# A state-space stage: per-head scalings as copies on ScalarE

## The chip, the cores and the metric

The kernel runs on one core of one Trainium2 chip. The metric is device time in microseconds; lower is better. The core has TensorE (matmuls), VectorE, ScalarE, GpSimd and SyncE, each with an instruction queue of its own that runs in order.

## The reference, cut to what matters

One layer of a hybrid encoder for a prompt of 1024 frames and for a running stream of 32 frames. One input projection feeds a state-space group of 8 heads (64 wide, two groups of four heads that share B and C of 128) and an attention group of 8 heads; both are joined by an output projection and followed by a gated feed-forward block.

```python
dt = softplus(dt_raw + dt_bias);  a = -exp(a_log)
da_cum = cumsum(dt * a)                               # inside a chunk
decay[q, s] = exp(da_cum[q] - da_cum[s])  for s <= q  # per head
scores = einsum('cqhn,cshn->cqsh', cm, bm) * decay
y_diag = einsum('cqsh,cshp->cqhp', scores, x * dt)
y_off  = einsum('cqhn,chpn,cqh->cqhp', cm, h_prev, exp(da_cum))
y = y_diag + y_off + d_skip[:, None] * xs
y = rmsnorm(y * silu(z), ssd_norm_g)
q, k = rmsnorm(q, q_norm_g), rmsnorm(k, k_norm_g)     # per head of 64
```

## The kernel before, in words

All matmuls that need it are made from two float32r halves, a rounded one and the rest, so each weight or activation is split: a cast to float32r and a subtraction. `split_unit` does that for weights, with the cast on ScalarE (L138) and the subtraction on GpSimd (L139).

The stage of interest runs from about 195 to 380 us. It merges two tracks, `merge(pieces[1:SSD_PIECES], chunks + ...)` (L618):

- `pieces`: the projection to v, k and q, by half and by pairs of 128-row tiles. A piece runs 2 x 24 matmuls of 256 columns into one of two PSUM banks of the tag "mm" (L153 to L155); ScalarE copies the bank to SBUF (L490). For q and k `qk_pair` then normalizes by head: square on ScalarE (L434), sum on VectorE (L436), `rsqrt` on GpSimd (L145, L146), two products on VectorE (L438, L439), and the split into `il`: the rounded half by a cast on GpSimd (L448), the rest by a subtraction on GpSimd (L449). One step later TensorE transposes `il` (L457), ScalarE copies the result to `st` (L460), and it is stored to DRAM for attention. v pieces are stored as they are.
- `chunks`: nine chunks of the scan, 128 rows each (the ninth is the stream's 32 rows). A chunk has five steps, one per turn, so that several chunks are under way. Step 1 loads `xb`, `bc`, `zz` and makes four `dm` tiles (128 x 4 x 128, float32r) on GpSimd: `upper`, the triangle of ones, times a per-partition, per-head scalar of `dAh` or `dAl` (L541). Step 2 sums them with `lowr` on TensorE (L548), takes the exponential on ScalarE (L551), masks the scores (L556, L560), and makes `xdt` on VectorE (L562), `xde` on GpSimd (L564) and `xd` on GpSimd: the inputs times `d_skip` of their head (L566). Steps 3 to 5 make the state (L575 to L589), the output (L595 to L602) and its transpose (L606 to L614).

`dm` has four buffers, just one chunk's worth, so a chunk's first `dm` waits for L548 of the chunk before; `xd` has two. Pools and buffers are given out by the Tile framework, which also sets each engine's order: it orders the instructions by a simulated timeline with the program's order as priority, and puts in the waits. DMAs are issued by SyncE. After the stage the remaining pieces (k and q of the second half) are merged with attention.

Of the kernel before, what the change touches and what calls it, by code (L numbers as in the profile page):

```python
# [7 lines left out]
F32 = mybir.dt.float32  # L8
# [3 lines left out]
AF = mybir.ActivationFunctionType  # L12
ALU = mybir.AluOpType
AX = mybir.AxisListType

P = 128
# [27 lines left out]
def build(tc, a):  # L44
    nc = tc.nc
# [26 lines left out]
    def nm(s):  # L72
        cnt[0] += 1
        return f"{s}_{cnt[0]}"
# [3 lines left out]
    def bank(tag, dt=F32):  # L78
        return ps.tile([P, 1024 if tag == "s" else 512], dt, tag=tag, bufs=BUFS[tag], name=nm("ps_" + tag))
# [62 lines left out]
    def rsqrt(pl, ss, n, rows, cols):  # L142
        m = pl.tile([P, cols], F32, tag=f"rs_m{cols}", bufs=2, name=nm("rs_m"))[:rows]
        r = pl.tile([P, cols], F32, tag=f"rs_r{cols}", bufs=2, name=nm("rs_r"))[:rows]
        nc.gpsimd.tensor_scalar(m, ss, 1.0 / n, EPS, op0=ALU.mult, op1=ALU.add)  # L145
        nc.gpsimd.tensor_tensor(r, m, mhalf[:rows, 0:cols], op=ALU.pow)  # L146
        return r

    def bc3(v, n):
        return v.unsqueeze(2).broadcast_to([v.shape[0], v.shape[1], n])  # L150
# [111 lines left out]
    dtb, alog, dsk = crow[:, 0:8], crow[:, 8:16], crow[:, 16:24]  # L262
# [19 lines left out]
    upper = cq.tile([P, P], F32, name="upper")  # L282
# [145 lines left out]
    def qk_pair(raw, tp, rows, g, hs, is_k):  # L428

        nt = raw.shape[1]  # L430
        r3 = raw.rearrange("p t h d -> p (t h) d")
        sq = p1.tile([P, 512], F32, tag="sq", bufs=1, name=nm("sq"))
        s3 = sq[:rows, 0:nt * 256].rearrange("p (h d) -> p h d", d=64)
        nc.scalar.activation(s3, r3, AF.Square)  # L434
        ss = p1.tile([P, 8], F32, tag="ss8", name=nm("ss8"))
        nc.vector.tensor_reduce(ss[:rows, 0:4 * nt], s3, axis=AX.X, op=ALU.add)  # L436
        r = rsqrt(p1, ss[:rows, 0:4 * nt], 64, rows, 4 * nt)
        nc.vector.tensor_tensor(r3, r3, bc3(r, 64), op=ALU.mult)  # L438
        nc.vector.tensor_tensor(r3, r3, g[:rows].unsqueeze(1).broadcast_to([rows, 4 * nt, 64]), op=ALU.mult)  # L439
        hc = slice(hs * 256, hs * 256 + 256)  # L440
        if is_k:
            if nt == 1:
                nc.sync.dma_start(a["o_ks"][:, hc], raw.rearrange("p t h d -> p (t h d)"))
            elif tp >= 2:
                nc.sync.dma_start(a["o_kp"][(tp - 2) * 256:(tp - 1) * 256, hc].rearrange("(t p) c -> p t c", p=P),
                                  raw.rearrange("p t h d -> p t (h d)"))
        il = p1.tile([P, 8, 2, 64], F32R, tag="il", name=nm("il"))
        nc.gpsimd.tensor_copy(il[:rows, 0:4 * nt, 0, :], r3)  # L448
        nc.gpsimd.tensor_tensor(il[:rows, 0:4 * nt, 1, :], r3, il[:rows, 0:4 * nt, 0, :], op=ALU.subtract)  # L449
        yield  # L450
        st = p1.tile([P, 4, 2 * P], F32R, tag="st", name=nm("st"))
        sf = st.bitcast(F32)
        hd = slice(4 * hs, 4 * hs + 4)
        for k in range(nt):
            tb = bank("t", F32R)
            for j in range(4):
                nc.tensor.transpose(tb[:, j * rows:(j + 1) * rows],  # L457
                                    il[:rows, 4 * k + j, :, :].rearrange("p a d -> p (a d)"), idr[:rows, :rows])
            tv = tb[:, 0:4 * rows].rearrange("p (j c) -> p j c", j=4)
            nc.scalar.copy(out=st[:, :, k * rows:(k + 1) * rows], in_=tv)  # L460
        c0, n = (2 * tp * P, 2 * P) if nt == 2 else (SB, NS)
        if is_k:
            nc.sync.dma_start(kst_d[hd, :, c0:c0 + n].rearrange("h p c -> p h c"), sf[:, :, 0:n])
        else:
            nc.sync.dma_start(qst_d[:, hd, 0, c0:c0 + n], sf[:, :, 0:n])
            nc.sync.dma_start(qst_d[0:64, hd, 1, c0:c0 + n], sf[64:128, :, 0:n])
            nc.sync.dma_start(qst_d[64:128, hd, 1, c0:c0 + n], sf[0:64, :, 0:n])

    class Slot:
# [10 lines left out]
        def piece(self, tp):  # L480
            hs, kind = self.hs, self.kind
            hc = slice(hs * 256, hs * 256 + 256)
            if tp == 4:
                rw, rows = self.rs, NS
            else:
                pb = bank("mm")
                for k in range(2):
                    tok_gemm(self.units, pb, 2 * tp + k, 256 * k)
                rw, rows = p1.tile([P, 2, 4, 64], F32, tag="raw", name=nm("rw")), P
                nc.scalar.copy(out=rw.rearrange("p t h d -> p (t h d)"), in_=pb)  # L490
            if tp == 2 and self.next:
                self.next.load()
            if kind:
                yield from qk_pair(rw, tp, rows, gk if kind == 1 else gq8, hs, kind == 1)
                return
            rf = rw.rearrange("p t h d -> p t (h d)")
            if tp == 4:
                nc.sync.dma_start(v_d[SB:NT, hc], rf[:, 0, :])
                nc.sync.dma_start(a["o_vs"][:, hc], rf[:, 0, :])
            else:  # L500
                pt_ = "(t p) c -> p t c"
                nc.sync.dma_start(v_d[tp * 256:(tp + 1) * 256, hc].rearrange(pt_, p=P), rf)
                if tp >= 2:
                    nc.sync.dma_start(a["o_vp"][(tp - 2) * 256:(tp - 1) * 256, hc].rearrange(pt_, p=P), rf)
# [16 lines left out]
    def v3(x_):  # L521
        return x_.rearrange("p (h d) -> p h d", h=8)

    def ssd_chunk(c):
        rows = P if c < 8 else NS
# [10 lines left out]
        xs = xb[:, 0:512]  # L536
        dms = []
        for d in (dAh, dAl):
            for g in range(2):
                dm = p3.tile([P, 4, P], F32R, tag="dm", bufs=4, name=nm("dm"))  # L540
                nc.gpsimd.tensor_tensor(dm, upper.unsqueeze(1).broadcast_to([P, 4, P]),  # L541
                                        bc3(d[:, c, 4 * g:4 * g + 4], P), op=ALU.mult)
                dms.append(dm)
        yield
        sg = bank("s")
# [17 lines left out]
        xde = p3.tile([P, 512], F32, tag="xde", bufs=1, name=nm("xde"))  # L563
        nc.gpsimd.tensor_tensor(v3(xde), v3(xdt), bc3(de[:, c, :], 64), op=ALU.mult)  # L564
        xd = p3.tile([P, 512], F32, tag="xd", name=nm("xd"))
        nc.gpsimd.tensor_tensor(v3(xd), v3(xs), bc3(dsk, 64), op=ALU.mult)  # L566
        yield
        if c == 8:
            st_in = p3.tile([P, 512], F32, tag="h", name=nm("h"))
# [45 lines left out]

    states = {-1: None}
    chunks, chunks_end = pipelined([ssd_chunk(c) for c in range(9)])
    merge(pieces[1:SSD_PIECES], chunks + [lambda: None])  # L618
    chunks_end()
# [695 lines left out]
```

## Time and profile before

| | |
|---|---|
| median of 3 runs | 1361.01 us (1359.01 to 1367.7) |
| profiled execution | 1365.81 us, span 1364.1 us |
| mean granted TensorE clock | 0.977 |
| TensorE busy | 1286.8 us (94%) |
| VectorE busy | 904.8 us (66%) |
| ScalarE busy | 502.6 us (37%) |
| GpSimd busy | 616.6 us (45%) |

How to read it: times of rows are those of one profiled execution. PE is TensorE's matmuls, PEld its weight loads, DVE is VectorE, ACT ScalarE, POOL GpSimd. A matmul's recorded time covers its pipelined run, so consecutive matmuls overlap in the record and a busy TensorE is not one at its peak. Idle time counts only on an engine that others wait for. Waits are put down to what released them last.

### The profile page before, as it was taken

Reading aid. Unit: us, or ns where it says so; the run is one execution under the profiler, and the core shown is the slowest. Engines: PE = TensorE matmul, PEld = TensorE weight load, DVE = VectorE, ACT = ScalarE, POOL = GpSimd, SP = SyncE. Lnnn points to the kernel's source line nnn. Section 1 sums busy time; section 2 is a strip of 40 time slices with the busy share of each in tenths; the row PEclk is TensorE's granted clock in tenths of the full one; section 3 lists DMA queues with packets and bytes.
Section 4 is the critical chain, followed back from the end, with each engine's and each line's share of the span. In section 5 each row is a group of like instructions: output and inputs, shape, how many; then the busy total and the mean of one; then the engine's idle time right before and its main releaser. Section 6 shows DMA issues by size and latency. Waiting matters only on the chain.

```text
span 1364.1 us, 23795 instructions
## 1 busy us (share of the span) xinstructions
PE 1286.8 (94%) x9260; PEld 1172.2 (86%) x9260; DVE 904.8 (66%) x1271; ACT 502.6 (37%) x865; POOL 616.6 (45%) x507
## 2 busy tenths in 40 slices
PE   5999999977899899999599999999999997999998
PEld 4999999967888688688599999999999995777777
DVE  5346446785747555665966677676676766667886
ACT  6235332322237543553533343333343335111210
POOL 7142248987636210220324455434455433345585
PEclk9999999978999999999799999999999999999999
DMA  7265252445375987665134454444454468668755
GB/s 270 76 206 161 90 171 66 151 134 182 121 212 178 335 285 225 194 202 173 68 94 136 146 171 139 131 136 133 148 171 138 132 213 295 234 229 306 254 189 204
DMA packets 201600, 242.02 MB, mean 177 GB/s; under 512 B 25840, under 2 KB 163120, under 8 KB 201488
## 3 DMA queue, kind: packets, MB, share of 16 engines
q1 hardware_dynamic: 201488, 240.51, 55.0%
q8 instruction: 73, 1.20, 0.4%
q14 instruction: 39, 0.32, 0.1%
HBM read 149.47 MB, written 90.99 MB: 176 GB/s over the span
## 4 chain that ended last, share of the span: by engine, by line
PE 66%; POOL 7%; DVE 7%; DMA 6%; issue 6%; ACT 1%; SPq 1%; DVEq 0%; ACTq 0%; POOLq 0%
PE ps_w L970 33%; PE ps_z L1171 11%; PE ps_mm L153 3%; PE ps_mm L154 3%; PE ps_mm L155 3%; PE ps_mm L162 2%; PE ps_mm L160 2%; PE ps_mm L161 2%; PE ps_mm L734 1%; PE ps_t L717 1%; POOL dm L541 1%; PE ps_s L695 1%; DMA qst_d<-st 1%; POOL rs_r L146 1%; DVE Z L1176 1%
## 5 line engine op out<-in xcount | busy, mean ns | idle before, releaser
L970 PE MATMUL ps_w<-T,whi 128*128 128x264 f32 x1408 | 229.5, 285 | 6.6 <-ACT T L918 5.9
L970 PEld LDWEIGHTS ps_w<-T,whi 128*128 128x128 f32 x1408 | 195.6, 189 | 7.2 <-ACT T L918 6.3
L978 DVE TENSOR_TENSOR sc<-sc,ps_w 128x528 f32<-128x528 f32 x154 | 105.3, 698 | 75.9 <-PE ps_w L970 73.9
L153 PE MATMUL ps_mm<-whi,hT_hi 128*128 128x256 f32 (+1 forms) x512 | 149.9, 293 | 5.5 <-ACT hT_hi L227 3.3
L155 PE MATMUL ps_mm<-whi,hT_lo 128*128 128x256 f32 (+1 forms) x512 | 149.4, 292 | 0.4 <-DVE hT_lo L228 0.4
L154 PE MATMUL ps_mm<-wlo,hT_hi 128*128 128x256 f32 (+1 forms) x512 | 149.3, 292 | 0.0
L970 PE MATMUL ps_w<-T,wlo 128*128 128x264 f32 x704 | 144.3, 287 | 0.0
L139 POOL TENSOR_TENSOR wlo<-raw,whi 128x1024 fp32r<-128x1024 f32 (+1 forms) x32 | 80.9, 2537 | 136.1 <-ACT whi L138 124.7
L946 ACT CAST whi<-raw 128x1024 fp32r<-128x1024 f32 x88 | 82.7, 941 | 99.7 <-PE ps_w L970 85.0
L1176 DVE TENSOR_TENSOR Z<-ps_z,Z 128x512 f32<-128x512 f32 x140 | 92.8, 685 | 37.2 <-PE ps_z L1171 30.5
L970 PE MATMUL ps_w<-fA,whi 128*128 128x264 f32 x704 | 116.3, 288 | 0.0
L947 DVE TENSOR_TENSOR wlo<-raw,whi 128x1024 fp32r<-128x1024 f32 x88 | 107.6, 1225 | 6.2 <-ACT whi L946 3.9
L1013 DVE TENSOR_TENSOR sc<-sc 128x512 fp32r<-128x512 f32 x77 | 77.7, 1019 | 48.7 <-ACT sc L1012 26.5
L970 PEld LDWEIGHTS ps_w<-T,wlo 128*128 128x128 f32 x704 | 109.8, 190 | 0.0
L153 PEld LDWEIGHTS ps_mm<-whi,hT_hi 128*128 128x128 f32 x512 | 100.2, 196 | 7.1 <-ACT hT_hi L227 3.7
L155 PEld LDWEIGHTS ps_mm<-whi,hT_lo 128*128 128x128 f32 x512 | 100.4, 196 | 1.8 <-DVE hT_lo L228 0.8
L154 PEld LDWEIGHTS ps_mm<-wlo,hT_hi 128*128 128x128 f32 x512 | 100.1, 196 | 0.3
L970 PEld LDWEIGHTS ps_w<-fA,whi 128*128 128x128 f32 x704 | 99.8, 191 | 0.4 <-PE ps_w L1064 0.4
L1171 PE MATMUL ps_z<-whi,fA 128*128 128x512 f32 x276 | 97.5, 391 | 0.0
L1012 ACT CAST sc<-sc 128x512 fp32r<-128x512 f32 x77 | 46.8, 621 | 111.5 <-DVE sc L1002 69.9
L954 POOL TENSOR_TENSOR raw<-raw,raw 128x512 f32<-128x512 f32 x22 | 37.2, 1690 | 91.1 <-DVE wlo L947 91.1
L970 PE MATMUL ps_w<-fA,wlo 128*128 128x264 f32 x352 | 72.2, 287 | 0.0
(284 smaller groups left out, 3099.6 us busy)
## 6 DMA issues: line engine op xcount, KB each, us to landing
act_d<-sc SPq DMA_DIRECT2D x154, 256.0 KB, 2.9
fA<-act_d SPq DMA_DIRECT2D x36, 896.0 KB, 6.3
raw<-in_wgu_dram SPq DMA_DIRECT2D x44, 512.0 KB, 3.6
raw<-in_wd_dram SPq DMA_DIRECT2D x22, 512.0 KB, 4.4
x<-in_xp_dram SPq DMA_DIRECT2D x16, 512.0 KB, 7.1
q<-qst_d SPq DMA_DIRECT2D x32, 256.0 KB, 4.6
mx<-mix_d SPq DMA_DIRECT2D x16, 512.0 KB, 4.5
raw<-in_wq_dram SPq DMA_DIRECT2D x14, 512.0 KB, 4.8
```

Of the source, the lines that this page charges most:

```text
L139: (eng or nc.gpsimd).tensor_tensor(lo, raw, hi, op=ALU.subtract)
L153: nc.tensor.matmul(ps_, lhsT=lh, rhs=rh, start=start, stop=False)
L154: nc.tensor.matmul(ps_, lhsT=lh, rhs=rl, start=False, stop=False)
L155: nc.tensor.matmul(ps_, lhsT=ll, rhs=rh, start=False, stop=stop)
L946: nc.scalar.copy(out=t[0][:, 0:w], in_=src)
L947: nc.vector.tensor_tensor(t[1][:, 0:w], src, t[0][:, 0:w], op=ALU.subtract)
L970: nc.tensor.matmul(out[:, h, :], lhsT=A[x][:, kb, :], rhs=B[:, y, kb, h * Q:(h + 1) * Q], start=(n == 0), stop=(n == len(terms) - 1))
L978: add = lambda o, x, y: nc.vector.tensor_tensor(o, x, y, op=ALU.add)
L1012: nc.scalar.copy(out=hi.bitcast(F32R), in_=src)
L1013: nc.vector.tensor_tensor(lo.bitcast(F32R), src, hi, op=ALU.subtract)
L1171: nc.tensor.matmul(pb, lhsT=at[k][:, q, x, :], rhs=bops[n0 + k][name][y], start=(i == 0), stop=(i == len(terms) - 1))
L1176: eng.tensor_tensor(o, x, y, op=ALU.add)
```

## The change

Three places, all of which take work from GpSimd and give it to ScalarE. The rounded half of `il` becomes a ScalarE copy. Each `dm` tile, one GpSimd product of 128x512, becomes four ScalarE copies of 128x128 with a per-partition scale, 16 a chunk. Each `xd`, one GpSimd product of 128x512, becomes eight scaled copies of 128x64. The subtraction into `il` stays on GpSimd.

```diff
         il = p1.tile([P, 8, 2, 64], F32R, tag="il", name=nm("il"))
-        nc.gpsimd.tensor_copy(il[:rows, 0:4 * nt, 0, :], r3)
+        nc.scalar.copy(out=il[:rows, 0:4 * nt, 0, :], in_=r3)
         nc.gpsimd.tensor_tensor(il[:rows, 0:4 * nt, 1, :], r3, il[:rows, 0:4 * nt, 0, :], op=ALU.subtract)
...
                 dm = p3.tile([P, 4, P], F32R, tag="dm", bufs=4, name=nm("dm"))
-                nc.gpsimd.tensor_tensor(dm, upper.unsqueeze(1).broadcast_to([P, 4, P]),
-                                        bc3(d[:, c, 4 * g:4 * g + 4], P), op=ALU.mult)
+                for k in range(4):
+                    nc.scalar.activation(dm[:, k, :], upper, AF.Copy, scale=d.bitcast(F32)[:, c, 4 * g + k:4 * g + k + 1])
                 dms.append(dm)
...
         xd = p3.tile([P, 512], F32, tag="xd", name=nm("xd"))
-        nc.gpsimd.tensor_tensor(v3(xd), v3(xs), bc3(dsk, 64), op=ALU.mult)
+        for h in range(8):
+            nc.scalar.activation(v3(xd)[:, h, :], v3(xs)[:, h, :], AF.Copy, scale=dsk[:, h:h + 1])
         yield
```

## Rows read from the trace of the kernel before

**Rows 1.** The page, GpSimd's busy tenths in 40 slices of 34.1 us.

```profile
POOL 7142248987636210220324455434455433345585
```

**Rows 2.** Busy us (instructions) of PE, PEld, DVE, ACT, POOL by stretch; clock, DMA, GB/s.

```profile
195.00:222.00 27.00, 27.00 (x215) 25.31 (x213) 15.61 (x16) 9.73 (x13) 26.67 (x24) 1.00 0.49 163
274.00:298.00 24.00, 15.01 (x82) 12.66 (x81) 19.29 (x16) 6.09 (x11) 19.93 (x23) 0.72 0.42 126
310.00:327.00 17.00, 10.11 (x65) 9.91 (x64) 4.16 (x4) 3.08 (x5) 9.15 (x8) 0.70 0.59 173
362.00:377.00 15.00, 11.32 (x69) 10.91 (x68) 10.42 (x17) 4.24 (x9) 9.23 (x11) 0.77 0.24 93
195.00:375.00 180.00, 158.74 (x1198) 148.71 (x1197) 126.58 (x142) 54.69 (x93) 150.00 (x138) 0.92 0.45 142
```

**Rows 3.** TensorE's waits, 195 to 385 us: total us, times, longest.

```profile
PE ps_t L457 <- POOL il L449: 8.3, 3, 6.9
PE ps_t L606 <- DVE y L602: 6.0, 2, 4.5
PE ps_t L457 <- DVE yt L613: 3.4, 1, 3.4
```

**Rows 4.** GpSimd's groups, 195 to 375 us: busy us, mean ns, idle before.

```profile
L541 POOL TENSOR_TENSOR dm<-upper,dAl 128x512 fp32r<-128x512 f32 x18 | 21.1, 1186 | 0.0
...
L541 POOL TENSOR_TENSOR dm<-upper,dAh 128x512 fp32r<-128x512 f32 x16 | 19.3, 1223 | 0.2
...
L566 POOL TENSOR_TENSOR xd<-xb,crow 128x512 f32<-128x512 f32 x9 | 10.0, 1113 | 2.8 <-ACT xd L600 2.8
L448 POOL CAST il<-rw 128x512 fp32r<-128x512 f32 x9 | 6.6, 735 | 6.9 <-DVE rw L439 5.4 <-ACT sq L434 1.4
```

**Rows 5.** GpSimd's timeline: start us, us, instruction and count.

```profile
282.23 2.03 POOL L541 TENSOR_TENSOR dm<-upper,dAh 128x512 fp32r<-128x512 f32 x2
...
285.44 2.03 POOL L541 TENSOR_TENSOR dm<-upper,dAl 128x512 fp32r<-128x512 f32 x2
...
304.13 2.82 POOL L541 TENSOR_TENSOR dm<-upper,dAh 128x512 fp32r<-128x512 f32 x2
306.91 2.48 POOL L541 TENSOR_TENSOR dm<-upper,dAl 128x512 fp32r<-128x512 f32 x2
309.35 1.07 POOL L448 CAST il<-rw 128x512 fp32r<-128x512 f32 x1
...
310.90 5.08 POOL L139 TENSOR_TENSOR wlo<-raw,whi 128x1024 fp32r<-128x1024 f32 x2
...
316.50 2.51 POOL L449 TENSOR_TENSOR il<-rw,il 128x512 fp32r<-128x512 f32 x2
```

**Rows 6.** VectorE: two products in the timeline; L438's least, median, longest ns.

```profile
273.62 2.28 DVE L560 TENSOR_TENSOR e<-e,gm 128x512 f32<-128x512 f32 x1
...
280.66 8.36 DVE L438 TENSOR_TENSOR rw<-rw,rs_r 128x512 f32<-128x512 f32 x1
...
L438 DVE TENSOR_TENSOR rw<-rw,rs_r x16: 671/1074/8356, 222.6 to 444.4; 128x512 f32<-128x512 f32 x16
```

**Rows 7.** ScalarE: groups by form over the whole run; two neighbours in the timeline.

```profile
L946 ACT CAST whi<-raw 128x512 fp32r<-128x512 f32 x22 | 13.6, 620 | 56.6 <-PE ps_w L970 56.6
...
L720 ACT COPY pt<-ps_t 128x128 f32<-128x128 f32 x16 | 4.2, 264 | 15.0 <-PE ps_t L717 7.5 <-PE ps_t L725 7.5
...
L707 ACT ACTIVATE pr<-ps_s,st 128x128 f32<-128x128 f32 x8 | 2.9, 370 | 7.5 <-DVE st L705 7.1 <-PE ps_t L725 0.4
...
L818 ACT COPY fR<-ps_t 128x64 f32<-128x64 f32 x4 | 0.7, 222 | 0.0
...
111.59 0.23 ACT L403 ACTIVATE eq<-ps_t 128x72 f32<-128x72 f32 x1
111.72 0.23 ACT L403 ACTIVATE de<-ps_t 128x72 f32<-128x72 f32 x1
```

**Rows 8.** ScalarE's waits, 195 to 375 us: total us, times, longest.

```profile
ACT rw L490 <- POOL il L449: 33.3, 7, 10.8
```

## Prediction

> **What bounds the kernel now.** Begin with the page's row of GpSimd by slices: in the five slices from 204 to 375 us it reads 8, 9, 8, 7, 6, while in the rest of the run it is mostly between 2 and 5 [rows 1]. That is the state-space stage, where chunks of the scan are merged with pieces of the q, k and v projection. Next, busy times by stretch: over 195 to 375 us GpSimd is busy 150.0 of 180 us, VectorE 126.6, ScalarE only 54.7, and TensorE 158.7 at a granted clock of 0.92 [rows 2]. TensorE is still the engine by which the stage is to be measured, and what it loses there is what there is to win. Its losses lie in three places: idle 24 - 15.01 = 9.0 us in 274 to 298, 17 - 10.11 = 6.9 us in 310 to 327, 15 - 11.32 = 3.7 us in 362 to 377, together 19.6 us. Around each it runs for a while at its lower level (1.2 instead of 2.4 GHz); busy time multiplied by what is missing from the clock is 15.01 x 0.28 = 4.2, 10.11 x 0.30 = 3.0 and 11.32 x 0.23 = 2.6 us, 9.8 us in all [rows 2]. So 29.4 us stand to be won, 2.2% of the run.
>
> Third, who ended TensorE's waits: GpSimd's `il` subtraction 8.3 us, VectorE's `y` 6.0 us and VectorE's `yt` 3.4 us [rows 3]. The two on VectorE lead back to GpSimd. One VectorE product of 128x512 (L438) takes 0.67 us at the least and took 8.36 us from 280.66 on; another (L560) took 2.28 us [rows 6]. GpSimd had four `dm` products (2.03 + 2.03 us) inside those 8.36 us. And the 6.9 us wait ends at the `il` subtraction of 316.50, in front of which GpSimd worked without a pause through four `dm` (2.82 + 2.48 us), a cast (1.07 us) and two weight splits (5.08 us) [rows 5].
>
> **The change, part by part.**
>
> *Taken from GpSimd.* In 195 to 375 us: `dm` 21.1 + 19.3 us, `xd` 10.0 us, casts of full `il` tiles 6.6 us [rows 4], together 57 of its 150 us. It falls to about 93 of 180 and stops being a bound. Place by place:
> - 310 to 327 us: ahead of the subtraction at 316.50 go 2.82 + 2.48 + 1.07 us, and a second cast and an `xd` of some 0.7 and 1.1 us by their means [rows 4, 5]: 8.2 us, more than the wait of 6.9. The wait and the low clock behind it go, 9.9 us. The cast comes back on ScalarE in the same chain at 0.62 us [rows 7]. Gain 9.3 us.
> - 274 to 298 us: L560 loses its 1.6 us of stretch, which sits in the chain to the wait on `y`, and GpSimd's queue ahead of that chain's reciprocal root gets shorter: I take 2.0 us. From L438 go at least the 4.1 us of the four `dm`, more than the 3.4 us that TensorE waited behind it, and some 0.6 us of smaller waits: 4.0. With two thirds of the idle 9.0 us gone I take 2.5 of the 4.2 us of low clock. Gain 8.5 us.
> - 362 to 377 us: only the last chunk's `xd` and one cast leave GpSimd, its other work stays: 2.0 of 6.3 us.
>
> Sum: 19.8 us. What is late next is VectorE's own chain through a chunk, and GpSimd's splits.
>
> *Added to ScalarE.* The trace has no copy with a scale read per partition from SBUF, so its price is bounded. A plain 128x128 copy out of PSUM takes 264 ns, an activation of that size that reads one operand per partition 370 ns, a 128x64 copy 222 ns; the operand thus costs 106 ns. Two short activations in a row start 0.13 us apart though the first takes 0.23, so 0.10 us overlaps [rows 7]. Middle values: 0.37 - 0.10 = 0.27 us for a `dm` slice, 0.222 + 0.106 - 0.10 = 0.23 us for an `xd` slice. Per chunk 16 x 0.27 + 8 x 0.23 = 4.3 + 1.8 us; for nine chunks 38.9 + 16.6 = 55 us. If the operand's read is hidden altogether it is 0.16 and 0.12 us, 32 us; if nothing overlaps 0.37 and 0.33 us, 77 us. I take the middle, since the overlap is seen in a row and the hiding of an operand is not. Casts in the stage: nine full ones at 0.62 us and three of 32 rows, 7 us. ScalarE goes from 55 to 117 us (94 to 139) in a stage that would last about 160: 73% (59 to 87%). It is not the bound, but its queue is in order and also empties the projection's banks (L490). The cover is the second bank: a bank takes 48 matmuls at 27.00 / 215 = 0.126 us [rows 2], 6.0 us. A full batch of `dm` and the copy itself, 4.3 + 0.6 us, fits under that; with a batch of `xd` as well, 6.7 us, it does not. I charge 3.5 us for the stage (five of the eight later chunks with 0.7 us each); the bounds are nothing, and 38 us by the slower rival below.
>
> *Waits that are new on ScalarE.* The `il` cast waits for VectorE's L439, and the first `dm` of a chunk for TensorE's L548 of the chunk before, since four buffers hold just one chunk. Behind either stand L490, the exponential (L551) and the copies to `st`, for all of which TensorE waits later. In exchange ScalarE's own waits for GpSimd's `il`, 33.3 us in seven times [rows 8], get shorter; I let the two cancel.
>
> *The casts of the later pieces* lie beside attention, where GpSimd is busy 6 tenths or less [rows 1]; I count nothing for either side there.
>
> The sum: 19.8 - 3.5 = 16 us. The profiled execution took 1365.8 us, so 1349.5; it lies 4.8 us over the median of 1361.0, and the forecast against that median is 1345.
>
> *A rule weighed.* L438 was held far longer than any one GpSimd instruction: 8.36 us [rows 6] against means of 1.1 to 1.2 us for a 128x512 product there [rows 4]. The Trainium skill (SBUF — State Buffer, "Who interferes with whom") says that a VectorE instruction with two SBUF inputs and a GpSimd instruction that reads SBUF exclude each other, whichever issued first, for the whole of that instruction. By that rule a stretch would end with one GpSimd instruction, and taking `dm` away would leave the wait of 3.4 us to some other cause. The row says that a run without a pause holds VectorE on. The measurement decides here; what the rule would make of the time is near the first rival.
>
> **Rivals.**
> 1. *Only the wait that ended directly on GpSimd goes.* The gain is the 9.3 us of 310 to 327; the waits on `y` and `yt` stay, VectorE's chain being held by something else. For it: they are VectorE's in the waits [rows 3], and splits, `e` and `xde` still run on GpSimd. Against it: the `dm` products inside L438. Time: 1361.0 - 9.3 + 3.5 = 1355.
> 2. *All of it goes.* ScalarE's work hides wholly and VectorE's chain shortens everywhere: 1361.0 - 29.4 = 1332. For it: ScalarE idles 125 us in the stage [rows 2]. Against it: the last chunk's chain keeps most of its GpSimd work.
> 3. *Slower: ScalarE's queue holds up TensorE's banks.* Place: L490 behind a chunk's batches. Price: 4.3 + 1.8 + 0.6 us, and a wait for VectorE amid them of half of what ScalarE's waits for `il` last now (33.3 / 7 = 4.8, so 2.4) [rows 8], is 9.1 us against a cover of 6.0: 3.1 us in each of eight chunks, 25 us. Idle time drew 9.8 / 19.6 = half of itself in lower clock [rows 2], so 38 us; less the 19.8 won, 18 us slower: 1379. It decides from the point where L490 comes more than 6.0 us after its bank's last matmul. Against it: slices of 0.27 us let other work in between, and ScalarE has a quarter of the stage to spare.
>
> **How the numbers follow.** A measurement of this kernel can tell about 1%, 13.6 us, from no change: below 1347 is faster, above 1375 slower. Chances: my forecast 0.42 (its own range 1337 to 1353, some seven tenths of it below 1347), rival 1 0.26, rival 2 0.16, rival 3 0.16. Faster: 0.42 x 0.7 + 0.16 = 0.45, and 0.03 for a first rival that also loses a third of the other waits, 0.48. Slower: 0.16. Within 1%: 0.36. The range reaches past the full recovery below and leaves out most of rival 3: 1329 to 1370.
>
> **What would show it.** Right: GpSimd near 95 us in the stage and ScalarE near 115; a `dm` slice about every 0.27 us; no `il` wait of TensorE over 2 us; L438 never above 4 us; a granted clock above 0.95 from 195 to 360; attention starting about 16 us sooner. Wrong: TensorE's waits now ended by ScalarE's L490 or L551 with several us each; `il` subtractions late behind a ScalarE cast; the low clock still there with the idle time gone; or a stage that is shorter and a later one that gives it back.

## The result and the profile after

The changed kernel takes 1353.88 us (median of 9 runs, 1351.48 to 1356.66) against 1362.17 us for the kernel before on the same chip (9 runs, 1359.01 to 1370.96). The ratio is 0.9927, 95% interval 0.9909 to 0.9946: about 10 us, 0.7%, faster. The profiled execution took 1352.69 us, its span 1350.9 us, its granted clock 0.981.

Line numbers from L567 on are one higher than before. First the stage by stretches, in the columns of [rows 2]:

```profile
274.00:298.00 24.00, 23.48 (x186) 21.59 (x185) 17.63 (x26) 20.15 (x63) 10.24 (x12) 1.00 0.68 216
310.00:327.00 17.00, 17.00 (x139) 16.56 (x138) 9.68 (x13) 11.15 (x33) 6.28 (x8) 1.00 0.56 173
362.00:377.00 15.00, 10.61 (x77) 10.17 (x75) 4.56 (x8) 3.20 (x7) 5.54 (x13) 0.89 0.80 249
195.00:375.00 180.00, 172.22 (x1355) 163.77 (x1348) 111.86 (x152) 117.46 (x316) 101.97 (x98) 0.97 0.49 157
```

The two large holes of before are full and at full clock. Over 180 us GpSimd is busy 102.0 us and ScalarE 117.5. TensorE's waits of 195 to 385 us, as in [rows 3], confirm it:

```profile
PE ps_s L700 <- DMA q<-qst_d: 3.3, 2, 1.7
PE ps_mm L153 <- ACT rw L490: 2.8, 1, 2.8
PE ps_t L596 <- DVE y L598: 2.4, 1, 2.4
PE ps_t L457 <- POOL il L449: 0.8, 1, 0.8
```

The first two now stand at the turn into attention, not amid the scan. VectorE's L438 on 128x512 had lasted 8.36 us in the kernel before, from 280.66 us on [rows 6]. Beside it GpSimd went through one unbroken run, the four `dm` of [rows 5] and these:

```profile
280.00 1.03 POOL L564 TENSOR_TENSOR xde<-xdt,de 128x512 f32<-128x512 f32 x1
281.00 1.26 POOL L560 TENSOR_TENSOR e<-e,gm 128x512 f32<-128x512 f32 x1
...
284.22 1.25 POOL L449 TENSOR_TENSOR il<-rw,il 128x512 fp32r<-128x512 f32 x1
...
287.43 1.03 POOL L566 TENSOR_TENSOR xd<-xb,crow 128x512 f32<-128x512 f32 x1
```

Now it stays below 2 us (least, median, longest in ns):

```profile
L438 DVE TENSOR_TENSOR rw<-rw,rs_r x16: 670/693/1787, 222.3 to 426.7; 128x512 f32<-128x512 f32 x16
```

The new instructions on ScalarE, in the timeline (start, length, eight in a row) and as groups of 195 to 375 us:

```profile
190.51 2.45 ACT L542 ACTIVATE dm<-upper,dAh 128x128 fp32r<-128x128 f32 x8 [4.17 <-DMA bc_d<-xc]
...
195.67 2.02 ACT L567 ACTIVATE xd<-xb,crow 128x64 f32<-128x64 f32 x8
```

```profile
L542 ACT ACTIVATE dm<-upper,dAl 128x128 fp32r<-128x128 f32 x66 | 20.9, 389 | 0.0
L542 ACT ACTIVATE dm<-upper,dAh 128x128 fp32r<-128x128 f32 x64 | 19.6, 388 | 3.6 <-PE ps_s L548 3.6
L567 ACT ACTIVATE xd<-xb,crow 128x64 f32<-128x64 f32 x72 | 18.2, 338 | 0.1
```

One slice lasts 0.39 and 0.34 us, but neighbours overlap: (2.45 - 0.389) / 7 = 0.29 us from start to start for `dm`, (2.02 - 0.338) / 7 = 0.24 us for `xd`.

So what was aimed at was reached, and yet a good part of it is missing at the end. To see where, count TensorE's instructions from 8 us on to three points in time. Columns as in [rows 2]; the second busy number with its count is PE's. Before:

```profile
8.00:340.00 332.00, 307.15 (x2248) 293.42 (x2249) 191.44 (x198) 126.83 (x217) 190.38 (x169) 0.96 0.46 148
8.00:380.00 372.00, 343.34 (x2514) 327.63 (x2515) 222.02 (x237) 138.68 (x240) 216.63 (x195) 0.95 0.45 144
8.00:470.00 462.00, 425.15 (x3229) 396.62 (x3230) 277.15 (x396) 188.18 (x365) 253.57 (x243) 0.96 0.51 163
```

After:

```profile
8.00:340.00 332.00, 321.60 (x2445) 308.73 (x2446) 180.98 (x212) 192.70 (x447) 140.58 (x122) 1.00 0.49 157
8.00:380.00 372.00, 353.18 (x2660) 338.91 (x2660) 205.98 (x251) 203.84 (x476) 164.40 (x151) 0.99 0.49 157
8.00:470.00 462.00, 433.55 (x3314) 403.74 (x3315) 266.07 (x416) 259.53 (x616) 192.66 (x179) 0.97 0.55 176
```

At 340 us the changed kernel is 197 TensorE instructions ahead, at 380 us 146, at 470 us 85. At some 0.126 us each (215 in 27.00 us [rows 2]) that is 25, 18 and 11 us. The stage gained 25 us; 14 of them were given back around the turn into attention, and the last number is close to the measured gain. (The records lack a few matmuls, so a count is good to some ten.)

### The profile page after: what moved, and what is told of

Read it like the earlier page. It is cut to its first block, busy times and chain, and to the rows that moved or that the text cites. A ratio compares the mean times of both kernels' runs of the same rounds, so it can differ in the third digit from the quotient of the medians.

```text
span 1350.9 us, 23952 instructions
## 1 busy us (share of the span) xinstructions
PE 1284.2 (95%) x9260; PEld 1170.1 (87%) x9260; DVE 887.6 (66%) x1271; ACT 568.7 (42%) x1101; POOL 552.1 (41%) x442
## 4 chain that ended last, share of the span: by engine, by line
PE 73%; DVE 7%; POOL 5%; issue 5%; DMA 5%; ACT 2%; SPq 1%; POOLq 0%; ACTq 0%; DVEq 0%
PE ps_w L971 33%; PE ps_z L1172 12%; PE ps_mm L153 4%; PE ps_mm L154 4%; PE ps_mm L155 4%; POOL rs_r L146 2%; PE ps_mm L162 2%; PE ps_mm L160 2%; PE ps_mm L161 2%; PE ps_mm L735 2%; PE ps_t L718 1%; PE ps_s L696 1%; PE ps_s L700 1%; DMA mix_d<-ot 1%; DVE Z L1177 1%
## 5 line engine op out<-in xcount | busy, mean ns | idle before, releaser
L971 PE MATMUL ps_w<-T,whi 128*128 128x264 f32 x1408 | 229.6, 285 | 4.9 <-ACT T L919 4.0
L153 PE MATMUL ps_mm<-whi,hT_hi 128*128 128x256 f32 (+1 forms) x512 | 149.0, 291 | 6.0 <-ACT hT_hi L227 3.2
L153 PEld LDWEIGHTS ps_mm<-whi,hT_hi 128*128 128x128 f32 x512 | 98.7, 193 | 8.0 <-ACT hT_hi L227 3.6
```

The costliest lines, as they stand in the source:

```text
L153: nc.tensor.matmul(ps_, lhsT=lh, rhs=rh, start=start, stop=False)
L971: nc.tensor.matmul(out[:, h, :], lhsT=A[x][:, kb, :], rhs=B[:, y, kb, h * Q:(h + 1) * Q], start=(n == 0), stop=(n == len(terms) - 1))
```

## The experiments

In the order in which they ran. Ratios are to the kernel before, timed on the same chip in the same session.

**Each part alone.** Three kernels that make one of the three edits on the kernel before, and the kernel before as a control.

> Only the dm products move to ScalarE; xd and the il casts stay on GpSimd. Theory A (dm was what made GpSimd's runs unbroken, and those runs held VectorE and the il subtraction): most of the change's 8 to 10 us, 1352 to 1356 us, no il wait of TensorE over 3 us, L438 at most 4 us. Rival B (the il cast in GpSimd's queue was the wait that mattered): a third of it or less, 1358 to 1362 us, with il waits of several us left. GpSimd's busy time from 195 to 375 us falls from 150 to about 108 by both.

```diff
-                nc.gpsimd.tensor_tensor(dm, upper.unsqueeze(1).broadcast_to([P, 4, P]),
-                                        bc3(d[:, c, 4 * g:4 * g + 4], P), op=ALU.mult)
+                for k in range(4):
+                    nc.scalar.activation(dm[:, k, :], upper, AF.Copy, scale=d.bitcast(F32)[:, c, 4 * g + k:4 * g + k + 1])
```

Measured: 1345.65 us, ratio 0.9856 (0.9812 to 0.9900).

> Only the xd products move to ScalarE. Theory A: 0 to 3 us faster, 1358 to 1362 us, since 10 us less in GpSimd's queue do not break its runs up. Rival C (any 10 us off GpSimd count the same, so the gain goes by its busy time): 10 of 57 us of the relief, about 1.7 us faster, and the il-only kernel the same.

```diff
-        nc.gpsimd.tensor_tensor(v3(xd), v3(xs), bc3(dsk, 64), op=ALU.mult)
+        for h in range(8):
+            nc.scalar.activation(v3(xd)[:, h, :], v3(xs)[:, h, :], AF.Copy, scale=dsk[:, h:h + 1])
```

Measured: 1351.35 us, ratio 0.9909 (0.9880 to 0.9937).

> Only the casts of il move to ScalarE. Theory A: within 3 us of the kernel before, 1358 to 1364 us, because the cast gives up a place in GpSimd's queue but now makes ScalarE wait for VectorE's L439. Rival B: most of the change's gain, 1353 to 1356 us.

```diff
-        nc.gpsimd.tensor_copy(il[:rows, 0:4 * nt, 0, :], r3)
+        nc.scalar.copy(out=il[:rows, 0:4 * nt, 0, :], in_=r3)
```

Measured: 1352.58 us, ratio 0.9919 (0.9893 to 0.9944).

> The kernel before once more, for a second profile of it. If the first profile, 3.6 us above the median of nine runs, held larger stalls than the usual run, the stretch from the first L548 to the last L606 (196.9 to 381.4 us, 184.5 us there) comes out 2 to 6 us shorter here, with at least one of the stalls of 4.5, 3.4 and 6.9 us smaller. If the excess lies elsewhere, it comes out at 184 to 185 us with the same three stalls.

This one has no edit. Measured: 1363.77 us, ratio 1.0010 (0.9993 to 1.0026). The stretch from the first L548 to the last L606 is 182.2 us instead of 184.5, but with the same three stalls (4.5, 3.4 and 6.9 us): they belong to the kernel and not to one profile.

Each part alone gains as much as all three together, or more: 1.4, 0.9 and 0.8% against 0.7%. All three times lie below every range that was expected for them, by theory A, B or C (the cast's only by half a microsecond). The load of GpSimd doesn't order them: here are the rows of 195 to 375 us of the kernel with `dm` alone, and below it with the cast alone; the last of the five busy times is GpSimd's.

```profile
195.00:375.00 180.00, 171.01 (x1342) 163.43 (x1339) 117.60 (x153) 95.18 (x231) 120.11 (x119) 0.96 0.51 161
```

```profile
195.00:375.00 180.00, 167.69 (x1327) 159.42 (x1326) 128.08 (x150) 63.75 (x112) 148.63 (x137) 0.96 0.48 154
```

The cast alone leaves GpSimd at 148.6 us, 1.4 less than before [rows 2] (its casts are gone, but more of the projection fell into the same 180 us), and takes 11 us off the time. TensorE's wait for `il`, 8.3 us before [rows 3], is still there with it:

```profile
PE ps_t L457 <- POOL il L449: 8.2, 2, 5.3
```

**Does any other order do the same, and what do two parts do?** The framework orders each engine by a simulated timeline, so every edit also deals the stage's order anew. Three kernels change only where `xd` is written, and one takes `dm` and `xd` together.

> The kernel before with the xd product written ahead of the xde product, all work on the same engines; the framework puts out another order of the stage. Theory A (the gain is GpSimd's relief): no change, 1361 to 1365 us, GpSimd busy 150 us from 195 to 375 us and its three long stalls of TensorE in some form. Theory O (the order of before holds three unlucky meetings, and any edit that deals the order anew loses them): 5 to 12 us faster, 1351 to 1358 us, with GpSimd just as busy.

```diff
-        xde = p3.tile([P, 512], F32, tag="xde", bufs=1, name=nm("xde"))
-        nc.gpsimd.tensor_tensor(v3(xde), v3(xdt), bc3(de[:, c, :], 64), op=ALU.mult)
         xd = p3.tile([P, 512], F32, tag="xd", name=nm("xd"))
         nc.gpsimd.tensor_tensor(v3(xd), v3(xs), bc3(dsk, 64), op=ALU.mult)
+        xde = p3.tile([P, 512], F32, tag="xde", bufs=1, name=nm("xde"))
+        nc.gpsimd.tensor_tensor(v3(xde), v3(xdt), bc3(de[:, c, :], 64), op=ALU.mult)
```

Measured: 1364.32 us, ratio 0.9993 (0.9981 to 1.0006).

> The kernel before with the xd product written ahead of the masking product gm; again the same work in another order. Theory A: 1361 to 1365 us. Theory O: 1350 to 1360 us, and not the same time as the other reordered kernel.

```diff
+        xd = p3.tile([P, 512], F32, tag="xd", name=nm("xd"))
+        nc.gpsimd.tensor_tensor(v3(xd), v3(xs), bc3(dsk, 64), op=ALU.mult)
         gm = p3.tile([P, 2, P], F32, tag="gm", bufs=1, name=nm("gm"))
...
-        xd = p3.tile([P, 512], F32, tag="xd", name=nm("xd"))
-        nc.gpsimd.tensor_tensor(v3(xd), v3(xs), bc3(dsk, 64), op=ALU.mult)
```

Measured: 1362.86 us, ratio 0.9995 (0.9981 to 1.0009).

> The changed kernel with the eight xd copies written ahead of xde; the same work in another order. Theory A: 1352 to 1356 us like the changed kernel. Theory O: anywhere from 1344 to 1358 us, as the 8 us between the changed kernel and dm alone would then be order too.

```diff
-        xde = p3.tile([P, 512], F32, tag="xde", bufs=1, name=nm("xde"))
-        nc.gpsimd.tensor_tensor(v3(xde), v3(xdt), bc3(de[:, c, :], 64), op=ALU.mult)
         xd = p3.tile([P, 512], F32, tag="xd", name=nm("xd"))
         for h in range(8):
             nc.scalar.activation(v3(xd)[:, h, :], v3(xs)[:, h, :], AF.Copy, scale=dsk[:, h:h + 1])
+        xde = p3.tile([P, 512], F32, tag="xde", bufs=1, name=nm("xde"))
+        nc.gpsimd.tensor_tensor(v3(xde), v3(xdt), bc3(de[:, c, :], 64), op=ALU.mult)
```

Measured: 1351.11 us, ratio 0.9905 (0.9887 to 0.9924). That is inside theory O's range and just under A's; its interval overlaps that of the changed kernel, so it tells nothing apart.

> dm and xd on ScalarE, the casts of il on GpSimd. If the cast's wait for VectorE in ScalarE's queue is what the changed kernel loses against dm alone: 1344 to 1348 us. If the xd copies are (18 us of ScalarE in the stage): 1350 to 1354 us. Theory O: no telling within 1344 to 1356 us.

This is the change without its first line; the cast stays on GpSimd:

```diff
-        nc.scalar.copy(out=il[:rows, 0:4 * nt, 0, :], in_=r3)
+        nc.gpsimd.tensor_copy(il[:rows, 0:4 * nt, 0, :], r3)
```

Measured: 1362.99 us, ratio 0.9994 (0.9978 to 1.0011). It lies outside all three ranges.

The first two don't disturb the three stalls of before and don't move the time, so "any edit helps" falls, at least for edits this small. `dm` and `xd` together gain nothing although GpSimd is busy only 105.1 us in the stage: theory A, by which GpSimd's load sets the time, falls with it. The timelines of ScalarE at the start of the stage show a first cost. With `dm` and `xd`:

```profile
191.69 2.46 ACT L542 ACTIVATE dm<-upper,dAh 128x128 fp32r<-128x128 f32 x8 [4.09 <-DMA bc_d<-xc]
194.06 2.43 ACT L542 ACTIVATE dm<-upper,dAl 128x128 fp32r<-128x128 f32 x8
...
196.86 2.02 ACT L567 ACTIVATE xd<-xb,crow 128x64 f32<-128x64 f32 x8
...
199.25 2.03 ACT L567 ACTIVATE xd<-xb,crow 128x64 f32<-128x64 f32 x8
...
207.53 1.03 ACT L551 ACTIVATE e<-ps_s 128x1024 f32<-128x1024 f32 x1
...
232.42 0.59 ACT L490 COPY rw<-ps_mm 128x512 f32<-128x512 f32 x1 [8.64 <-POOL il L449]
...
242.86 1.03 ACT L551 ACTIVATE e<-ps_s 128x1024 f32<-128x1024 f32 x1 [2.06 <-PE ps_t L596]
```

With `dm` alone:

```profile
190.58 2.45 ACT L542 ACTIVATE dm<-upper,dAh 128x128 fp32r<-128x128 f32 x8 [4.48 <-DMA bc_d<-xc]
...
202.59 1.02 ACT L551 ACTIVATE e<-ps_s 128x1024 f32<-128x1024 f32 x1
...
229.63 1.03 ACT L551 ACTIVATE e<-ps_s 128x1024 f32<-128x1024 f32 x1 [2.08 <-PE ps_t L595]
```

Two batches of `xd`, 4.0 us, which nobody needs yet, stand ahead of the first exponential, and it starts 4.9 us later (1.1 us of it was there from the first `dm` on). By the third chunk the exponential is at 242.9 instead of 229.6 us; in between ScalarE waited 8.64 us, in order, for GpSimd's `il`. From there to the ninth chunk the lag stays between 8 and 13 us.

**Is it the buffer of the projection?** ScalarE's copy L490 waits for `il` to release one of two `rw` buffers, 33.3 us in all [rows 8]. A third one, at the price of the second buffer of the small `smp` tiles, on three kernels.

> The kernel before with three buffers instead of two for the projection's rows (rw), paid for by one buffer instead of two for the stream's 32 rows (smp). Theory Q (a q or k piece holds its rw buffer from L490 to L449, through five hops over ScalarE, VectorE and GpSimd; with two of them full, ScalarE's L490 stops, both banks fill and TensorE runs out of projection work to put between the chunks' matmuls): L490's 33 us of waiting for il fall under 10 us, the stalls of 4.5, 3.4 and 6.9 us shrink to under 2 us each, 1346 to 1354 us. Theory A (GpSimd's load): GpSimd is as busy as before, so 1358 to 1364 us.

```diff
-            self.rs = p1.tile([NS, 1, 4, 64], F32, tag="smp", bufs=2, name=nm("smp"))
+            self.rs = p1.tile([NS, 1, 4, 64], F32, tag="smp", bufs=1, name=nm("smp"))
...
-                rw, rows = p1.tile([P, 2, 4, 64], F32, tag="raw", name=nm("rw")), P
+                rw, rows = p1.tile([P, 2, 4, 64], F32, tag="raw", bufs=3, name=nm("rw")), P
```

Measured: 1366.07 us, ratio 1.0010 (0.9992 to 1.0029). L490's wait for `il` fell only to 22.8 us, not under 10.

> The changed kernel with three rw buffers. Theory Q: little left to win in the stage, 1345 to 1354 us, and L490's 10 us of waiting for il nearly gone. Rival S (ScalarE's queue is what the changed kernel loses against dm alone): unchanged at 1351 to 1355 us.

The same two lines on the changed kernel. Measured: 1355.03 us, ratio 0.9945 (0.9927 to 0.9963). L490's wait went from 10.2 to 6.7 us; the time lies at the upper edge of rival S's range, no better than with two buffers.

> dm and xd on ScalarE, il casts on GpSimd, three rw buffers; with two it measured 1363 us. Theory Q: its stalls come from rw buffers waiting for il (17.8 us in L490), so 1345 to 1353 us. Rival S (the 18 us of xd copies make ScalarE late, and that cost the 17 us against dm alone): 1358 to 1364 us, no better than with two.

The same two lines on the kernel with `dm` and `xd`. Measured: 1358.64 us, ratio 0.9955 (0.9934 to 0.9976). L490's wait went from 17.8 to 2.9 us, but the time misses theory Q's range and lies in S's. By the ratios it is 0.4% better than with two buffers, between two sessions and with intervals that all but touch.

The first of these is a miss in time and the most telling run of all. TensorE's counts with the third buffer on the kernel before:

```profile
8.00:340.00 332.00, 314.66 (x2372) 301.18 (x2373) 200.57 (x202) 128.34 (x222) 195.82 (x171) 0.98 0.47 150
8.00:380.00 372.00, 349.35 (x2648) 334.74 (x2648) 231.04 (x243) 139.30 (x242) 224.40 (x199) 0.99 0.45 145
8.00:470.00 462.00, 420.22 (x3239) 392.85 (x3240) 285.36 (x401) 188.79 (x370) 258.66 (x243) 0.97 0.52 165
```

By 380 us it is 134 instructions, 17 us, ahead of the kernel before, nearly as far as the changed one (146). By 470 us 10 are left. TensorE worked more in the stage and nothing came of it. From 340 to 470 us it was idle for 24.4 us (130 less 420.22 - 314.66), against 12.0 in the kernel before and 18.1 in the changed one. What hardly moved is the start of attention. The first row is attention's exponential in the kernel before, the next two the third buffer and the changed kernel (least, median and longest ns, then the start of the first and of the last):

```profile
L707 ACT ACTIVATE pr<-ps_s,st x10: 360/592/703, 393.9 to 417.5; 128x128 f32<-128x128 f32 x2, 128x256 f32<-128x256 f32 x2, 128x384 f32<-128x384 f32 x2, 128x512 f32<-128x512 f32 x2
```

```profile
L707 ACT ACTIVATE pr<-ps_s,st x11: 360/589/811, 392.7 to 418.8; 128x128 f32<-128x128 f32 x2, 128x256 f32<-128x256 f32 x2, 128x384 f32<-128x384 f32 x2, 128x512 f32<-128x512 f32 x2
```

```profile
L708 ACT ACTIVATE pr<-ps_s,st x15: 358/681/810, 377.9 to 419.7; 128x640 f32<-128x640 f32 x5, 128x128 f32<-128x128 f32 x2, 128x256 f32<-128x256 f32 x2, 128x384 f32<-128x384 f32 x2
```

Nor did the end of the scan, the ninth chunk's last copy to `mixS`. In the kernel before, with the third buffer, and in the changed kernel:

```profile
381.44 0.29 DVE L609 COPY mixS<-ps_t 128x128 f32<-128x128 f32 x1 [0.35 <-PE ps_t L606]
```

```profile
381.23 0.29 DVE L609 COPY mixS<-ps_t 128x128 f32<-128x128 f32 x1 [0.58 <-PE ps_t L606]
```

```profile
365.70 0.29 DVE L610 COPY mixS<-ps_t 128x128 f32<-128x128 f32 x1 [0.84 <-PE ps_t L607]
```

That gives a theory C. The scan is a chain from chunk to chunk, and attention starts a fixed while after its end; the projection is filler in its gaps. A stage that fills better without a faster chain only uses up the filler, and TensorE then idles at the turn. All profiles bear on it. "Last dm" is the end of the last `dm` instruction, "scan's end" the end of the copy to `mixS` and "attention" the start of its first exponential (all from the timelines); "lead" is the count of TensorE instructions done by 470 us, less the 3229 of before:

| kernel | last dm, us | scan's end, us | attention, us | lead at 470 us | ratio |
|---|---|---|---|---|---|
| before | 337.2 | 381.7 | 393.9 | 0 | 1 |
| before again | 340.2 | 382.7 | 394.4 | -4 | 1.0010 |
| xd ahead of xde | 336.9 | 381.5 | 393.6 | -3 | 0.9993 |
| xd ahead of gm | 337.3 | 380.0 | 391.6 | 17 | 0.9995 |
| before, three rw | 329.3 | 381.5 | 392.7 | 10 | 1.0010 |
| dm and xd | 328.4 | 377.9 | 389.3 | 22 | 0.9994 |
| dm and xd, three rw | 331.3 | 378.6 | 388.6 | 29 | 0.9955 |
| after, three rw | 327.2 | 377.3 | 388.4 | 44 | 0.9945 |
| xd alone | 328.9 | 374.0 | 384.6 | 71 | 0.9909 |
| cast alone | 325.7 | 372.5 | 382.5 | 80 | 0.9919 |
| after, xd first | 325.3 | 370.4 | 382.4 | 65 | 0.9905 |
| after | 321.2 | 366.0 | 377.9 | 85 | 0.9927 |
| dm alone | 316.5 | 364.2 | 376.7 | 121 | 0.9856 |

Attention follows the last `dm` by 54 to 63 us in every one, and the scan's end much more closely, by 10 to 12.5 us. With the third buffer on the kernel before the last `dm` is 8 us sooner but the scan's end only 0.2 us: the later chunks lost it again, and attention went with the end. The ratios follow attention by and large. The changed kernel and `dm` with `xd` are slower than their places; so is the latter against itself with three buffers, whose scan ends 0.7 us later. What ties attention to the scan's end was not tested.

**The chain itself.** The last run lets the chain end sooner. Written as it is, the last chunk's steps 2 to 5 come after all pieces of the stage. Three empty turns put its steps 2 to 4 among the pieces, and they also bring the turns of all chunks closer together, since more of them are spread over the same pieces; only the fifth step still comes last. It was made on the kernel with `dm` alone, the fastest so far.

> dm alone on ScalarE, as in the run before of that kind (1345.7 us), and the last chunk's remaining steps are merged among the projection pieces instead of being written after all of them: three empty turns more behind the nine chunks. No work is added or moved to another engine. Theory C (the scan's chain sets the end: in the profiles so far attention's first exponential came 54 to 63 us after the end of the last dm, whatever TensorE had done of the projection by then, and the time followed it): the chunks are turned faster, the last dm ends well before 316 us, attention's first exponential comes before 372 us and the time is 1335 to 1342. Theory A (the load of GpSimd sets the stage): GpSimd's work of the stage is the same and only moved ahead, 1343 to 1349. Theory D (each edit deals the order anew and any stage comes out within some 10 us of another, with no chain that decides): 1345 to 1360, and attention's first exponential not tied to the last dm.

```diff
-    chunks, chunks_end = pipelined([ssd_chunk(c) for c in range(9)])
+    chunks, chunks_end = pipelined([ssd_chunk(c) for c in range(9)] + [iter(()) for _ in range(3)])
```

Measured: 1340.19 us (1339.48 to 1341.03, 4 runs), ratio 0.9817 (0.9763 to 0.9871): about 25 us faster than the kernel before and the fastest of all. The counts with `dm` alone:

```profile
8.00:340.00 332.00, 321.33 (x2453) 309.25 (x2453) 191.93 (x217) 174.31 (x374) 160.71 (x142) 1.00 0.49 158
...
8.00:470.00 462.00, 435.48 (x3350) 407.03 (x3350) 272.68 (x420) 233.92 (x525) 216.41 (x208) 0.98 0.55 176
```

With the empty turns, counts and attention's exponential:

```profile
8.00:340.00 332.00, 323.21 (x2444) 309.76 (x2444) 189.49 (x224) 173.49 (x375) 160.01 (x147) 0.99 0.49 158
...
8.00:470.00 462.00, 440.47 (x3404) 410.06 (x3405) 266.43 (x431) 238.45 (x533) 214.38 (x210) 0.98 0.56 181
```

```profile
L707 ACT ACTIVATE pr<-ps_s,st x18: 367/708/811, 355.0 to 416.1; 128x640 f32<-128x640 f32 x8, 128x128 f32<-128x128 f32 x2, 128x256 f32<-128x256 f32 x2, 128x384 f32<-128x384 f32 x2
```

At 340 us both are as far as each other (2444 and 2453), and GpSimd's and ScalarE's work is the same, so TensorE won nothing in the stage. But the scan ends 20 us sooner:

```profile
343.82 0.29 DVE L609 COPY mixS<-ps_t 128x128 f32<-128x128 f32 x1 [0.43 <-PE ps_t L606]
```

Attention starts 21.7 us sooner, 57.0 us behind the last `dm` (298.0 us) and 10.9 us behind the scan's end, while pieces are still left to fill the turn. Of L153 alone, with `dm` alone and then with the empty turns:

```profile
8.00:340.00 332.00, 123.28 (x427) 81.36 (x427) 1.00 0.49 158
```

```profile
8.00:340.00 332.00, 119.59 (x412) 78.77 (x412) 0.99 0.49 158
```

The lead at 470 us is 175 instead of 121. The time lies in theory C's range (1335 to 1342) and under those of A and D. (The two kernels with `dm` on ScalarE were not timed side by side, and their intervals overlap; the counts at 470 us tell them apart more clearly than the ratios.) Attention's 21.7 us gave only some 5.5 us of time. TensorE's idle time from 340 to 470 us went from 15.9 to 12.7 us, so there was little to fill: starting sooner seems worth no more than the idle time that it fills.

## Why the prediction was right, and where not

The forecast was 1345 us in a range of 1329 to 1370; 1353.9 us lies in the range, and a gain of 0.7% is "within 1%", the second of the three cases (0.36), not the likeliest. That the time lies in the range is in part luck: the stage won more than the sum had, 25 us for 16, and a loss that the sum did not have took 14 of them back.

- *GpSimd falls to about 93 us, ScalarE rises to 117.* Measured 102.0 and 117.5 us. ScalarE's price held: 0.29 and 0.24 us a slice against 0.27 and 0.23. The Trainium skill (ScalarE: Activation LUTs, "What ACT_TABLE_LOAD costs") gives 186 ns and 0.833 ns an element, 93 ns more for a pointer operand, and 93 ns of overlap between neighbours; the estimate from that page, 0.293 and 0.239 us, agrees with the trace better than the prediction's own. GpSimd's busy time is higher than forecast because more work fell into the same 180 us (1355 TensorE instructions against 1198).
- *310 to 327 us: 9.3 us, and 274 to 298 us: 8.5 us.* Both came, in full. TensorE is busy 17.00 of 17 and 23.48 of 24 us, at a clock of 1.00, and the wait on `il` is 0.8 us. With no run of `dm` beside it, L438 on 128x512 lasts 1.79 us at the most: there it began at 240.90 us, beside a GpSimd subtraction of 1.31 us from 240.83 on, and it ended at 242.69 although GpSimd's next instruction had followed at 242.10. The prediction weighed a rule of the Trainium skill (SBUF — State Buffer, "Who interferes with whom") and read it so that a stretch ends with one GpSimd instruction; by that reading the wait behind L438 would have stayed. The wait went, as the row of before had it. The exclusion itself is not contradicted by that. The traces show both, a hold over a whole run of GpSimd instructions before and one of about a single instruction after; why VectorE got in sooner there stays open. Here even the second rival (all of it goes, 29.4 us) was near: the lead at 340 us is 25 us.
- *362 to 377 us: 2.0 us.* This did not come. TensorE is busy 10.61 us of that stretch instead of 11.32, though it is now a different piece of work, the turn into attention, with 0.80 of the DMA engines busy.
- *ScalarE's queue costs 3.5 us.* Not where I looked for it. TensorE's one wait of size on L490 is 2.8 us at the turn. The third rival (1379 us) is refuted here. What the batches do delay is the first exponential: 206.3 us in the changed kernel, 202.6 with `dm` alone, 198.7 before. Against the kernel before that is made up by the third chunk (239.2 against 239.5 us). Against `dm` alone, whose last `dm` ends 4.7 us sooner, it may be what the chain lost, but no run shows it.
- *Attention starts about 16 us sooner.* It did: 377.9 against 393.9 us.

The step that failed is the sum itself: "16 us, so 1349.5". It takes TensorE time that is recovered in the stage for time at the end. The recovered time was filled with projection matmuls that the kernel before did after the stage. Of L153 alone, counted to 380 us, before and then after:

```profile
8.00:380.00 372.00, 128.11 (x436) 85.86 (x436) 0.95 0.45 144
```

```profile
8.00:380.00 372.00, 139.52 (x480) 92.51 (x480) 0.99 0.49 157
```

With the third buffer on the kernel before the count is 480 too; in the kernel before it gets there only at 400 us.

```profile
8.00:380.00 372.00, 137.97 (x480) 91.05 (x480) 0.99 0.45 145
```

They were missing at the turn. From 340 to 470 us the changed kernel did 869 TensorE instructions where the kernel before did 981, and 96 of L153 where that did 132. The prediction named "a stage that is shorter and a later one that gives it back" as a sign of error; it is what happened, for about 14 of 25 us. The first rival gave 1355 us, closest to the measurement, but by another way: the waits on `y` (L602) and `yt` that it kept did go.

That the end of the scan decides rather than GpSimd's load or TensorE's stalls is shown by the third buffer on the kernel before (17 us of lead at 380 us, the scan's end within 0.2 us of before, no gain) and, less sharply, by the empty turns (the same count at 340 us, the scan's end 20 us sooner, 54 instructions more at 470 us). For the changed kernel itself the empty turns were not tried; that it gives back for the same reason is argued from its counts. Open too is how the dealt order comes to slow the chain with `dm` and `xd` together: its later start accounts for 4.9 us of the 11.9 by which its last `dm` is late against `dm` alone, and the 8.64 us wait for `il` could account for the rest, in a single profile. And that the changed kernel is 0.7% behind `dm` alone with attention only 1.2 us later isn't explained; its granted clock from 380 to 400 us is 0.74 against 1.00, in single profiles.

## What to carry to other kernels

Where filler is merged into a latency chain, idle time that is won on the bound engine may be lost again unless the chain ends sooner too: look at the counts of its instructions at a later point, past the stage, before a gain is booked. Try the parts of a change alone, since they need not add up: here `dm` alone beats all three. And see that a chain's last steps aren't written behind all of the filler.

## What the runs showed that was not expected

The parts are not additive: `dm` alone -1.4%, `xd` alone -0.9%, the cast alone -0.8%, `dm` and `xd` together -0.1%, and all three -0.7%. In a kernel whose order is dealt anew by every edit, a single edit's gain may hold some luck of the order. How much was not shown: of the two smallest reorderings neither moved the time by more than 0.1%, and that of the changed kernel's `xd` by 0.2%, within the noise.
